# Gate and up products of the second layer's feed-forward stage in two by two blocks with seven half-size products

## Chip, cores, metric

The kernel runs on one core of one Trainium2 chip. The metric is the device time of one execution in microseconds (us). Before the change the median of three runs is 1883.36 us (1878.64 to 1889.82).

## The reference, cut to what matters

A two-layer backbone on 512 latent and 256 context tokens of width 1024. Each layer mixes tokens and then runs a feed-forward stage (FFN) with 2816 hidden columns. The last layer doesn't need its context tokens any more, so its FFN works on the 512 latent tokens alone.

```python
def swiglu(h, w_i, w_o):
    g, u = jnp.split(h @ w_i, 2, axis=-1)
    return (jax.nn.silu(g) * u) @ w_o
...
        xl = xl + ml[2] * rms_norm(yl, g[1])
        xl = xl + ml[5] * rms_norm(swiglu(adaln(xl, g[2], ml[3], ml[4]), w_ffn_in[l], w_ffn_out[l]), g[3])
```

All numbers are float32.

## The kernel before

**Three matmuls for one product.** TensorE runs in the float32r form. Every operand is kept as two parts: `hi`, the value as ScalarE rounds it to float32r, and `lo`, what is left, subtracted by VectorE. A product is hi·hi + hi·lo + lo·hi, so `mm3` issues three matmuls into one PSUM bank. TensorE wants 128 rows (kc runs over eight such blocks of the width 1024).

**Memory.** One SBUF arena is cut into regions, which the profile names reg0, reg1 and so on. In the second layer's FFN reg0 and reg1 hold the normed activations H2 (hi and lo), reg2 the products `silu(g)*u` of the four hidden blocks ("slots") of a group, hi and lo, reg3 scratch, reg4 and reg5 the output rows that are summed up over the groups, reg7 five weight slots (hi and lo, 1024 columns each) and reg8 three raw buffers for weights as they come from HBM, besides small things.

**Weights.** SyncE's queue (SP) fetches all weights through the three raw buffers in one fixed list (`build_seq`), 512 KB each. `pump` turns a raw buffer into a weight slot, in the list's order: ScalarE copies 1024 columns to hi, VectorE subtracts to lo, and the raw buffer goes to the next fetch. A weight slot comes free when its last matmul has been issued (`done`).

**The FFN** (`ffn`). The 22 hidden blocks are taken in groups of 4, 4, 4, 4, 2 and 4. For each block `unit` makes gate and up, each as 8 kc times 3 matmuls of 128x512 (48 for both), then silu on ScalarE, the multiply on VectorE, and the split into hi and lo. After the blocks of a group come its down products: for each of four tiles of 128 tokens and each half of 512 output columns, the group's blocks times three matmuls of 128x512. VectorE adds them to the output rows. The first group begins with two blocks in halves of 256 tokens, since their tiles come out of the stage ahead one by one. In the first layer the same is done for 768 tokens, as 512 and 256.

**The gates.** `gate` spreads the modulation column over rows: four transposes of 128x128 on TensorE into a spare bank, then a copy by ScalarE, for each half of 512. The first layer has four such steps (latent and context), the second two. They are queued at the fourth group.

**Order.** One Python generator emits TensorE's work, and side lanes emit the rest when a clock that the builder keeps says that it is due. What comes out is one fixed order on each engine, and each engine runs its own order strictly.

Of the kernel before, what the change touches and what calls it, by code (L numbers as in the profile page):

```python
# [18 lines left out]
CTX = 256  # L19
# [131 lines left out]
class Builder:  # L151
    def __init__(self, tc, ctx, ins, out):
# [7 lines left out]
        cuts = [A0, A0 + 6144, B0, B0 + 6144, C0, VB, X0, W0, RAW0, self.L.end]  # L160
        self.reg = [[a, b, None, None] for a, b in zip(cuts, cuts[1:])]
        for i, k in enumerate('rrfffffrf'):
            self.mode(i, k)
        self.M = gp.tile([128, 7, 128], U8, name="M")
# [6 lines left out]
        self.narrow = False  # L171
# [20 lines left out]
    def V(self, off, *dims, p0=0, np_=128):  # L192
        a, b, t = self.find(off)
        t0 = t[:, off - a:off - a + 1]
        ps = t0.ap[0][0]
        return bass.AP(t0.tensor, t0.offset + p0 * ps, [[ps, np_]] + [list(d) for d in dims])
# [26 lines left out]
    def mm(self, out, lhsT, rhs, start=True, stop=True):  # L223
        n, m = self.cols(rhs), self.cols(lhsT)
        if rhs.dtype == F32R:
            t = max(0.417 * n, 105)
# [9 lines left out]
        self.nc.tensor.matmul(out, lhsT, rhs, start=start, stop=stop)  # L236

    def mm3(self, out, lh, ll, rh, rl, start, stop):
        r = self.r
        self.mm(out, r(lh), r(rh), start, False)  # L240
        self.mm(out, r(lh), r(rl), False, False)
        self.mm(out, r(ll), r(rh), False, stop)
# [119 lines left out]
    groups = [4, 4, 4, 4, 2, 4]  # L362

    def build_seq(self):
# [15 lines left out]
        for l in range(DEPTH):  # L380
# [23 lines left out]
            for gi, g in enumerate(self.groups):  # L404
                for i in range(2 * f, 2 * (f + g)):
                    w(I['wfi'][l, i])
                    if l == 0 and i > 3 and spread:
                        raw(spread.pop(0), 'g')
                for i in range(f, f + g):
                    w(I['wfo'][l, i])  # L410
                if l == 0:
# [3 lines left out]
        self.seq, ns = [], 0  # L415
        for a, k in seq:
            self.seq.append([a, k, ns, None])
            ns += k == 'w'
# [5 lines left out]

    def pump(self, upto=-1):
        seq, go = self.seq, True
        while go:
            go = False
            if self.n_dma < len(seq) and self.slots:
                it = seq[self.n_dma]  # L430
                it[3] = RAW0 + self.slots.pop(0) * 1024
                self.dma(self.S(it[3], 1024), it[0])
                self.n_dma += 1
                go = True
            while self.n_proc < self.n_dma and seq[self.n_proc][1] != 'w':
                self.n_proc += 1
            if (self.n_proc < self.n_dma and seq[self.n_proc][2] < self.n_freed + NW
                    and (self.n_proc <= upto or self.ck.written(self.S(seq[self.n_proc][3], 1024)) <= self.now + 200)):
                it = seq[self.n_proc]
                w = W0 + (it[2] % NW) * 2048  # L440
# [1256 lines left out]
```

## Time and profile before

| what | value |
| --- | --- |
| median of three runs | 1883.36 us (1878.64 to 1889.82) |
| the profiled execution's own time | 1883.15 us |
| its span | 1881.0 us |
| TensorE (PE) busy | 1812.2 us, 96% |
| VectorE (DVE) busy | 1040.1 us, 55% |
| ScalarE (ACT) busy | 684.0 us, 36% |
| GpSimd (POOL) busy | 208.1 us, 11% |

Busy time of TensorE counts a matmul from its start to its modelled end, so that it says little of how fast matmuls follow each other. For that one counts them between two starts. The second layer's FFN reaches from about 1500 us to the end.

### The profile page before, as it was taken

The numbers are of one execution on the slowest core, as the hardware profiler recorded it, in microseconds if no ns is written. First come the engines' busy times: TensorE is split into PE (matmuls) and PEld (weight loads), VectorE is DVE, ScalarE is ACT, GpSimd is POOL, SyncE is SP. The second block draws the span as 40 slices with busy tenths as digits, with TensorE's granted clock in tenths as the row PEclk, the third lists the DMA queues.
The fourth block names the chain that finished last, engine by engine and source line by source line (L and its number), as shares of the span: only waits on it lengthen the run. The fifth ranks groups of instructions, "written<-read, shape, count | busy, mean of one in ns | idle before, by whom it ended". The sixth has DMA issues, their size and how long they took to land.

```text
span 1881.0 us, 27410 instructions
## 1 busy us (share of the span) xinstructions
PE 1812.2 (96%) x11140; PEld 1507.5 (80%) x11140; DVE 1040.1 (55%) x1781; ACT 684.0 (36%) x1374; POOL 208.1 (11%) x287
## 2 busy tenths in 40 slices
PE   6999999997999999999999999999998989999998
PEld 3888886676789888888888878888776788888886
DVE  3478853566475666555455374887476542433444
ACT  4533431357473221212212264333266543222222
POOL 0000003234220000000000040000434100000002
PEclk9999999998999999999999999999999999999999
DMA  9211118442123433434343212111431223243221
GB/s 343 68 57 35 35 53 202 143 83 62 52 106 99 148 124 112 149 120 144 110 144 107 68 45 72 52 46 57 90 79 33 69 88 101 70 121 101 90 90 56
DMA packets 52782, 179.88 MB, mean 96 GB/s; under 512 B 6960, under 2 KB 7856, under 8 KB 52656
## 3 DMA queue, kind: packets, MB, share of 16 engines
q1 hardware_dynamic: 48816, 169.48, 28.3%
q0 software_dynamic: 3840, 8.65, 3.3%
q8 instruction: 87, 1.43, 0.3%
q14 instruction: 39, 0.32, 0.1%
HBM read 167.36 MB, written 2.10 MB: 90 GB/s over the span
## 4 chain that ended last, share of the span: by engine, by line
PE 85%; DVE 5%; ACT 5%; DMA 2%; issue 1%; POOL 1%; SPq 0%; DVEq 0%; POOLq 0%; ACTq 0%
PE P L236 82%; PE P L246 3%; ACT reg1f L257 1%; ACT reg3f L257 1%; DVE reg8f L959 1%; ACT reg7r L257 1%; DVE reg7r L264 1%; ACT reg8f L257 1%; DMA reg4f<-in_wmod 0%; DMA reg8f<-in_wmod 0%; DMA reg0r<-reg5r 0%; DVE reg4f L264 0%; DMA reg8f<-in_wout 0%; ACT reg0r L257 0%; DVE reg8f L276 0%
## 5 line engine op out<-in xcount | busy, mean ns | idle before, releaser
L236 PE MATMUL P<-reg2r,reg7r 128*128 128x256 f32 (+1 forms) x1920 | 481.0, 338 | 0.2 <-ACT reg8f L257 0.2
L236 PE MATMUL P<-reg0r,reg7r 128*128 128x512 f32 (+1 forms) x1344 | 380.3, 363 | 3.9 <-ACT reg0r L257 3.9
L264 DVE TENSOR_TENSOR reg7r<-reg8f,reg7r 128x1024 fp32r<-128x1024 f32 x200 | 243.1, 1225 | 232.7 <-ACT reg7r L257 231.1
L236 PEld LDWEIGHTS P<-reg2r,reg7r 128*128 128x128 f32 x1920 | 330.2, 190 | 39.1 <-issue 0.7
L257 ACT ACTIVATE reg7r<-reg8f 128x1024 fp32r<-128x1024 f32 x204 | 212.8, 1053 | 369.0 <-issue 150.8
L236 PE MATMUL P<-reg7r,reg0r 128*128 128x512 f32 (+1 forms) x1272 | 328.5, 389 | 8.1 <-ACT reg0r L257 6.1
L236 PE MATMUL P<-reg3r,reg7r 128*128 128x512 f32 (+1 forms) x960 | 321.9, 335 | 0.4 <-DVE reg3r L264 0.4
L236 PEld LDWEIGHTS P<-reg0r,reg7r 128*128 128x128 f32 x1344 | 243.1, 191 | 52.5 <-issue 8.4
L236 PEld LDWEIGHTS P<-reg7r,reg0r 128*128 128x128 f32 x1272 | 233.2, 190 | 58.0 <-ACT reg0r L257 7.1
L236 PE MATMUL P<-reg1r,reg7r 128*128 128x512 f32 (+1 forms) x672 | 241.3, 359 | 0.6 <-DVE reg1r L264 0.6
L236 PE MATMUL P<-reg7r,reg2r 128*128 128x512 f32 (+1 forms) x912 | 231.4, 382 | 5.6 <-DVE reg3r L276 1.9
L236 PEld LDWEIGHTS P<-reg7r,reg2r 128*128 128x128 f32 x912 | 165.7, 188 | 39.4 <-ACT reg2r L257 2.3
L236 PEld LDWEIGHTS P<-reg3r,reg7r 128*128 128x128 f32 x960 | 182.4, 190 | 18.5 <-issue 0.7
L236 PEld LDWEIGHTS P<-reg1r,reg7r 128*128 128x128 f32 x672 | 128.3, 191 | 18.7 <-DVE reg1r L264 1.1
L276 DVE SCALAR_TENSOR_TENSOR reg8f<-reg8f 128x512 f32<-128x512 f32 (+3 forms) x154 | 87.6, 569 | 10.6 <-DMA reg8f<-in_wmod 7.7
L236 PE MATMUL P<-reg7r,reg1r 128*128 128x512 f32 (+1 forms) x240 | 90.6, 378 | 0.1
L959 DVE TENSOR_REDUCE reg8f<-P 128x1 f32<-128x768 f32 (+1 forms) x80 | 67.5, 846 | 30.3 <-PE P L236 30.1
L284 POOL TENSOR_TENSOR reg8f<-reg8f 128x1 f32<-128x1 f32 (+2 forms) x102 | 60.2, 592 | 182.5 <-ACT reg5f L257 98.5
L257 ACT ACTIVATE reg3f<-P,reg8f 128x768 f32<-128x768 f32 (+3 forms) x96 | 52.6, 569 | 59.2 <-DVE reg8f L959 46.8
L257 ACT ACTIVATE reg0r<-reg1f 128x256 fp32r<-128x256 f32 (+1 forms) x46 | 23.5, 511 | 135.4 <-DVE reg1f L264 135.4
L236 PE MATMUL P<-reg7r,reg3r 128*128 128x512 f32 (+1 forms) x192 | 70.0, 364 | 0.0
L257 ACT ACTIVATE reg3f<-P 128x512 f32<-128x512 f32 (+2 forms) x106 | 45.1, 442 | 65.5 <-PE P L246 34.7
(218 smaller groups left out, 2012.0 us busy)
## 6 DMA issues: line engine op xcount, KB each, us to landing
reg8f<-in_wfi SPq DMA_DIRECT2D x88, 512.0 KB, 3.6
reg8f<-in_wmod SPq DMA_DIRECT2D x80, 512.0 KB, 3.7
reg8f<-in_win SPq DMA_DIRECT2D x56, 512.0 KB, 3.6
reg8f<-in_wfo SPq DMA_DIRECT2D x44, 512.0 KB, 3.6
reg8f<-in_wout SPq DMA_DIRECT2D x16, 512.0 KB, 4.2
reg6f<-in_xin SPq DMA_DIRECT2D x12, 512.0 KB, 6.3
reg2r<-reg5r POOLq DMA_DIRECT2D x24, 192.0 KB, 6.0
reg2f<-in_wmod SPq DMA_DIRECT2D x8, 512.0 KB, 6.4
```

The costliest lines, as they stand in the source:

```text
L236: self.nc.tensor.matmul(out, lhsT, rhs, start=start, stop=stop)
L246: self.nc.tensor.transpose(out, in_, self.S(self.L.ident, 128))
L257: self.nc.scalar.activation(out=out, in_=in_, func=func, **kw)
L264: self.nc.vector.tensor_tensor(out=out, in0=a, in1=b, op=op)
L276: self.nc.vector.scalar_tensor_tensor(out=out, in0=a, scalar=s, in1=b, op0=op0, op1=op1)
L284: self.nc.gpsimd.tensor_tensor(out=out, in0=a, in1=b, op=op)
L959: self.nc.vector.tensor_reduce(out=sm(i, 2 + m), in_=x, axis=AX.X, op=ALU.min)
```

## The change

Three things change in the code.

**Blocks.** In the second layer (`fast = (1,)`), from the second group on, `pair` takes gate and up of a hidden block together as one product of a two by two block matrix (gate and up, by the two halves of the 1024 input columns) with another (the two halves of the input columns, by the two halves of 256 tokens). It is made with seven half-size products instead of eight (Winograd's form of Strassen's rule), each of 4 kc and 3 matmuls of 128x256: 84 for both gate and up. In PSUM three of them are added on top of a product that has been read already. Four sums of weight blocks (`sums`, and one in `split_s2`, 512 columns each) are made for every hidden block, and four sums of activation blocks (T1 to T4, `tblocks`) once. `sum2` gives a sum to POOL or to VectorE, as the builder's clock has it. A hidden block now takes four weight slots instead of two: the hi and lo splits are 3584 columns instead of 2048. T4 is written over a block that the first group still reads, so it is made when the second group begins.

**Splits.** For the whole program the lo subtraction is no longer emitted right behind the hi copy, but once the builder's clock has the copy done (`flush`), so VectorE's order changes in many places. Scratch and gate change places in the arena, and the regions are cut finer: reg7 is now reg9, reg8 is reg10, and in the second layer's FFN H2 lies in reg0 to reg2, the hidden blocks in reg3, T2 and the gate in reg4, scratch in reg5, the output rows in reg6 and reg7.

**Down products and gates.** The first tile of a group takes the last hidden block of both halves at its end, the last tile takes both halves side by side. The gates are queued in the last group: in the second layer within the last pair, in the first layer ahead of the last group's down products, where TensorE's own work waits until they are done.

```diff
+    fast = (1,)
...
+                seq.append((I['wfi'][l, i], 'ab'[i % 2] if gi and l in self.fast else 'w'))
...
+            elif k == 'b':
+                ab = [first, i]
+                self.task(0, self.split_a11, ab[:1])
+                self.task(None, self.sums, ab)
+                self.task(None, self.split_s2, ab)
+                self.task(0, self.split, ab[:1])
+                self.task(0, self.split_s4, ab[:1], ab[:1])
+                self.task(0, self.split, ab[1:], ab[1:])
...
+    def sum2(self, out, a, b, op):
+        n = self.cols(out)
+        if max(self.ck.t['po'], self.now) + 2.4 * n < max(self.ck.t['dv'], self.now) + 1.4 * n + 700:
+            self.pool(out, a, b, op, 2.36 * n)
+        else:
+            self.tt(out, a, b, op)
+    def sums(self, w, a, b):
+        a, b, tmp = self.raw(a), self.raw(b), self.S(self.L.u, 512)
+        a11, a21, a22 = self.S(a, 512), self.S(b, 512), self.S(b + 512, 512)
+        yield max(self.ck.written(self.S(k, 1024)) for k in (a, b)) if not self.lows else 1e12
+        self.sum2(a11, a11, a21, ALU.subtract)
+        self.sum2(tmp, a22, a11, ALU.subtract)
+        self.sum2(a21, a21, a22, ALU.add)
+    def split_s2(self, w, a, b):
+        tmp = self.S(self.L.u, 512)
+        yield self.ck.written(tmp)
+        self.halves(w, 512, tmp, 512, lambda: self.sum2(tmp, self.S(self.raw(a) + 512, 512), tmp, ALU.subtract))
...
+            t1 = self.S(TS + 1920, hw)
+            while self.n_t < 3:
+                yield self.now + 500
+            for kc in range(4):
+                diff(at(B21, kc), at(T2, kc))
+                yield self.ck.t['dv']
+                put(T4, kc, t1)
+                yield self.ck.t['dv']
+            self.n_t = 4
...
+            z = self.get()
+            ba, bb = self.bank(), self.bank()
+            yield from prod(z, B11, ba, True)
+            self.act(c1, self.B(ba, hw))
+            yield from prod(z + 512, T2, bb, True)
+            self.done()
+            if last:
+                self.mode(ra + 1, 'f')
+                self.sides[1].append(self.gate(l, 5, G5))
+            yield lambda: not slot or slot - 1 in mul_
+            self.tt(q6, c1, self.B(bb, hw), ALU.add)
+            y, w4, x = self.get(), self.get(), self.get()
+            bc = self.bank()
+            yield from prod(x, T1, bc, True)
+            yield lambda: not slot or put_.get(slot - 1) == 2
+            self.act(p5, self.B(bc, hw))
+            yield from prod(y + 512, B21, ba, False)
+            self.act(s1, self.B(ba, hw), AF.Silu)
+            yield from prod(y, T3, bb, False)
+            self.done()
+            self.tt(u3, c1, self.B(bb, hw), ALU.add)
+            yield from prod(w4, B22, bc, False)
+            self.done()
+            self.tt(q6, q6, self.B(bc, hw), ALU.add)
+            self.sides[2].append(late())
+            yield lambda: self.n_t == 4
+            bd = self.bank()
+            yield from prod(x + 512, T4, bd, True)
+            self.done()
+            self.tt(u3, u3, self.B(bd, hw), ALU.add)
+            self.tt(u3, u3, s1, ALU.mult)
+            self.sides[0].append(put(u3, 0))
...
-            if gi == 3:
-                self.sides[1].append(self.gate(l, 5, G5))
             if last:
-                while self.extra:
+                if not fast:
+                    self.mode(ra + 1, 'f')
+                    self.sides[1].append(self.gate(l, 5, G5))
+                while self.extra and not (fast and (1, 1, 1) in self.have):
                     self.more(force=True)
                 self.nbk = 6 if l else 5
                 yield lambda: not self.sides[1]
...
+                if t == order[0]:
+                    todo = [(nh, i) for nh in range(2) for i in range(g - 1)] + [(nh, g - 1) for nh in range(2)]
+                elif t == order[-1]:
+                    todo = [(nh, i) for i in range(g) for nh in range(2)]
```

`late()` in it adds u3 to p5 (by `sum2`), takes the silu of q6, multiplies, and splits the result into hi and lo; `put` splits.

What this does to the engines' orders is seen at three places. The first is VectorE for one hidden block in the middle of a group of the second layer's FFN. Before, reg3 is scratch, reg2 the hidden block, reg7 the weight slots, reg8 the raw buffers:

```order
L264 TENSOR_TENSOR reg3f<-reg3f,P 128x512
L264 TENSOR_TENSOR reg2r<-reg3f,reg2r 128x512
L264 TENSOR_TENSOR reg7r<-reg8f,reg7r 128x1024 x2
L264 TENSOR_TENSOR reg3f<-reg3f,P 128x512
L264 TENSOR_TENSOR reg2r<-reg3f,reg2r 128x512
```

After, with scratch in reg5, the hidden block in reg3, weight slots in reg9 and raw buffers in reg10:

```order
L267 TENSOR_TENSOR reg10f<-reg10f 128x512
L267 TENSOR_TENSOR reg3r<-reg5f,reg3r 128x256 x2
L267 TENSOR_TENSOR reg5f<-reg5f,P 128x256
L267 TENSOR_TENSOR reg9r<-reg10f,reg9r 128x512
L267 TENSOR_TENSOR reg9r<-reg10f,reg9r 128x1024
L267 TENSOR_TENSOR reg5f<-reg5f,P 128x256 x2
L267 TENSOR_TENSOR reg9r<-reg10f,reg9r 128x512
L267 TENSOR_TENSOR reg9r<-reg10f,reg9r 128x1024
L267 TENSOR_TENSOR reg5f<-reg5f 128x256
L267 TENSOR_TENSOR reg5f<-reg5f,P 128x256
L267 TENSOR_TENSOR reg5f<-reg5f 128x256
L267 TENSOR_TENSOR reg9r<-reg10f,reg9r 128x512
```

In place of four instructions a block VectorE has fourteen: one sum of raw weights, five lo splits of weights, four adds out of PSUM, two multiplies or adds in scratch and two lo splits of the block. The other three sums of 512, and one add of 256, stand on POOL.

The second place is VectorE in the first such block of the second group, which began before with the same rows as above. Now lo splits of T4 (written to reg1) and sums for it (out of reg2) stand among the block's own work:

```order
L267 TENSOR_TENSOR reg5f<-reg5f,P 128x256
L267 TENSOR_TENSOR reg9r<-reg10f,reg9r 128x512
L267 TENSOR_TENSOR reg5f<-reg5f,P 128x256
L267 TENSOR_TENSOR reg1r<-reg5f,reg0r 128x256
L267 TENSOR_TENSOR reg5f<-reg5f,reg2r 128x256
L267 TENSOR_TENSOR reg5f<-reg5f 128x256
L267 TENSOR_TENSOR reg1r<-reg5f,reg0r 128x256
L267 TENSOR_TENSOR reg3r<-reg5f,reg3r 128x256
```

The third row reads the bank of the block's sixth product; the last two of T4's four lo splits stand behind it, and the seventh product reads T4.

The third place is TensorE in the first layer, where the gates stand. Before, they lie among the down products of the fourth group (reg7 are weight slots, reg0 the hidden blocks, the 128x128 rows out of reg8 the transposes of the gate steps and one of the modulation's own):

```order
L246 MATMUL P<-reg8f 128x128 x4
L236 MATMUL P<-reg7r,reg0r 128x512 x6
L246 MATMUL P<-reg8f 128x128 x4
L236 MATMUL P<-reg7r,reg0r 128x512 x12
L246 MATMUL P<-reg8f 128x128 x4
L236 MATMUL P<-reg7r,reg0r 128x512 x108
```

After, they lie between the last group's hidden blocks and its down products (reg3 and reg5 are H2 in this layer, reg9 the weight slots, reg10 where the modulation lies):

```order
L239 MATMUL P<-reg5r,reg9r 128x256
L239 MATMUL P<-reg3r,reg9r 128x256
L249 MATMUL P<-reg10f 128x128 x16
L239 MATMUL P<-reg9r,reg0r 128x512 x72
L249 MATMUL P<-reg10f,reg2f 128x128 x8
```

The sixteen transposes of the four gate steps now stand in one piece, with no other matmul between them, and the down products of the last group wait behind them.

More of the change, by code (lines that the diff above doesn't have):

```diff
@@ L193, in V @@
         a, b, t = self.find(off)
+        assert off + sum((n - 1) * st for st, n in dims) < b
         t0 = t[:, off - a:off - a + 1]
@@ L423, in build_seq, with raw, halves, low @@
         self.n_hi = 0
+    def raw(self, k):
+        return self.seq[k][2]
+    def halves(self, w, o, x, n, then=None):
+        hi, lo = self.S(w + o, n), self.S(w + 1024 + o, n)
+        if self.n_proc >= self.n_hi:
+            self.act(self.r(hi), x)
+        def low():
+            if self.sides[2] and self.nbk == 2 and self.ck.t['po'] + 1200 < self.ck.t['dv']:
+                self.pool(self.r(lo), x, hi, ALU.subtract, 2.36 * n)
+            else:
+                self.tt(self.r(lo), x, hi, ALU.subtract)
+            if then:
+                then()
+        self.lows.append([hi, low, (), self.n_proc + 1])
@@ new lines, in flush, with task @@
+    def flush(self, upto):
+        while self.lows and (self.lows[0][3] <= upto or self.ck.written(self.lows[0][0]) <= self.now + 150):
+            _, low, frees, _ = self.lows.pop(0)
+            low()
+            for k in frees:
+                self.slots.append((self.raw(k) - RAW0) // 1024)
+    def task(self, new, fn, needs, frees=()):
+        if new is not None:
+            self.ends.append(0)
+        self.tasks.append((len(self.ends) - 1, fn, needs, frees))
+        self.ends[-1] = len(self.tasks)
@@ new lines, in ffn, with pair, soon, put @@
+        put_, mul_ = {}, set()
+        def pair(slot, last):
+            c1, q6, u3, p5, s1 = [self.S(TS + k * hw, hw) for k in range(5)]
+            at = A + slot * 1536 + o1
+            def soon(x):
+                return self.ck.written(x) - 250
+            def put(x, o):
+                hi, lo = self.S(at + o, hw), self.S(at + 768 + o, hw)
+                yield soon(x)
+                self.act(self.r(hi), x)
+                yield soon(hi)
+                self.tt(self.r(lo), x, hi, ALU.subtract)
+                put_[slot] = put_.get(slot, 0) + 1
+            def late():
+                self.sum2(p5, p5, u3, ALU.add)
+                yield soon(q6)
+                self.act(q6, q6, AF.Silu)
+                yield soon(q6)
+                self.tt(p5, p5, q6, ALU.mult)
+                mul_.add(slot)
+                yield from put(p5, hw)
+            def prod(w, b, bk, first):
+                yield self.ck.free(bk) if first else max(v for e, v in self.ck.bank.get(bk, {'pe': 0.0}).items())
+                for kc in range(4):
+                    self.mm3(self.B(bk, hw), self.S(w + kc * 128, 128), self.S(w + 1024 + kc * 128, 128),
+                             self.S(b[0] + b[1] * kc, hw), self.S(b[0] + b[1] * kc + b[2], hw), first and kc == 0, kc == 3, not first)
+                    if kc % 2:
+                        yield
+            z = self.get()
[30 more added lines that the diff above has]
+            self.sides[0].append(put(u3, 0))
@@ L1429, in ffn @@
                     self.more()
+        while self.extra:
+            self.more(force=True)
     def ffn_fin(self, t, yo, G5, TS, l, H):
```

257 lines of the change are left out of this document (174 added, 83 removed).

## The prediction

> **What bounds the kernel now.** I read the page first, then the second layer's FFN alone. On the page TensorE (PE) is busy nearly all the time at the full granted clock (PEclk in tenths, 40 slices):
>
> ```profile
> span 1881.0 us, 27410 instructions
> PE 1812.2 (96%) x11140; PEld 1507.5 (80%) x11140; DVE 1040.1 (55%) x1781; ACT 684.0 (36%) x1374; POOL 208.1 (11%) x287
> PEclk9999999998999999999999999999999999999999
> ```
>
> Busy time alone doesn't show that nothing is lost. So I took the FFN's stretch from 1540 to 1870 us in the view by windows, PE's waits in it, and its longest piece in the chain of waits:
>
> ```profile
> 1540.00:1870.00 330.00, 329.17 (x1455) 271.60 (x1454) 127.84 (x143) 90.81 (x120) 8.05 (x11) 1.00 0.30 94
> PE P L236 <- ACT reg2r L257: 0.8, 1, 0.8
> 1539.81 212.51 PE P L236 x937
> ```
>
> The columns of the first row are PE, weight load, DVE, ACT, POOL, clock, DMA. PE waits once, for 0.8 us, and otherwise 937 matmuls of 128x512 follow each other in 212.51 us: 0.2268 us each. DVE works 128 of 330 us, POOL 8. The stage is bound by the number and width of its matmuls, and the other engines have room. What the change saves on PE comes off the time, as long as nobody makes PE wait.
>
> **What the seven products save.** The new matmuls are 128x256. Such matmuls, with the same alternation of hi and lo weights, stand at the start of this stage, in the first halves (timeline of PE):
>
> ```profile
> 1503.23 0.28 PE L236 MATMUL P<-reg1r,reg7r 128*128 128x256 f32 x1
> ...
> 1507.91 0.28 PE L236 MATMUL P<-reg1r,reg7r 128*128 128x256 f32 x1
> ```
>
> Between these two lie 13 threes, 39 matmuls in 4.68 us: 0.120 us each. One hidden block cost 48 x 0.2268 = 10.89 us and will cost 84 x 0.120 = 10.08 us, 0.81 less. 18 of 22 blocks are taken this way: -14.5 us. That is all there is to gain, 0.8% of the time. It would be nothing at 0.1296 us a matmul (10.89 / 84).
>
> The Trainium skill (TensorE: Matmul & The Clock Gate, "Back-to-back issue gap") gives the isolated warm gap as N / 2.4 + 2.5 ns; by that estimate 109.2 and 215.8 ns would save 1.19 us a block and 21.3 us in all. The trace has about 11 ns more on either width, so the sum goes by its rows.
>
> **What DVE and POOL must do beside it.** Durations by form, with the idle time before each group behind the bar: 512 and 1024 columns on DVE and ACT and the fetches from 1540 to 1870 us, 256 columns on DVE from 1500 to 1533, POOL from the whole span:
>
> ```profile
> L264 DVE TENSOR_TENSOR reg7r<-reg8f,reg7r 128x1024 fp32r<-128x1024 f32 x58 | 70.3, 1224 | 80.6 <-ACT reg7r L257 80.6
> L264 DVE TENSOR_TENSOR reg2r<-reg3f,reg2r 128x512 fp32r<-128x512 f32 x20 | 13.9, 693 | 14.0 <-ACT reg2r L257 14.0
> L264 DVE TENSOR_TENSOR reg3f<-reg3f,P 128x512 f32<-128x512 f32 x20 | 13.7, 687 | 62.7 <-PE P L236 62.7
> L264 DVE TENSOR_TENSOR reg2r<-reg3f,reg2r 128x256 fp32r<-128x256 f32 x3 | 1.3, 425 | 1.5 <-ACT reg2r L257 1.5
> L264 DVE TENSOR_TENSOR reg3f<-reg3f,P 128x256 f32<-128x256 f32 x3 | 1.3, 419 | 9.4 <-PE P L236 7.5 <-ACT reg3f L257 2.0
> L257 ACT ACTIVATE reg7r<-reg8f 128x1024 fp32r<-128x1024 f32 x58 | 60.2, 1052 | 121.4 <-issue 85.6 <-PE P L236 18.0 <-DMA reg8f<-in_wfi 10.3
> L257 ACT ACTIVATE reg2r<-reg3f 128x512 fp32r<-128x512 f32 x20 | 12.6, 632 | 92.4 <-DVE reg3f L264 92.4
> L284 POOL TENSOR_TENSOR reg8f<-reg8f,reg6f 128x512 f32<-128x512 f32 x16 | 20.4, 1277 | 41.6 <-PE P L236 40.9
> L284 POOL TENSOR_TENSOR reg3f<-reg3f 128x256 f32<-128x256 f32 x4 | 2.9, 730 | 13.7 <-ACT reg8f L257 7.7 <-DVE reg3f L270 3.6 <-PE P L246 2.4
> reg8f<-in_wfi SPq DMA_DIRECT2D x36, 512.0 KB, 3.6
> ```
>
> By the order of the changed program a block gives DVE four adds out of PSUM (4 x 0.42 = 1.68 us), one sum of 512 (0.69), three lo splits of 512 and two of 1024 (2.08 + 2.45), and four of 256 in scratch and splits (1.70): 8.60 us, of which 6.92 with both inputs in SBUF. POOL gets three sums of 512 and an add of 256: 3 x 1.277 + 0.73 = 4.56 us. PE needs 10.08. Taken alone DVE fits, at 85%. They aren't alone. Three places in the timeline of attention show what happens when the two meet:
>
> ```profile
> 321.11 2.69 POOL L284 TENSOR_TENSOR reg8f<-reg8f,reg6f 128x512 f32<-128x512 f32 x2 [8.12 <-PE P L236]
> ...
> 322.04 0.81 DVE L264 TENSOR_TENSOR reg8f<-reg8f,reg6f 128x512 f32<-128x512 f32 x1
> ...
> 431.70 2.35 POOL L284 TENSOR_TENSOR reg7r<-reg8f,reg7r 128x1024 fp32r<-128x1024 f32 x1 [1.86 <-ACT reg7r L257]
> ...
> 432.73 1.33 DVE L276 SCALAR_TENSOR_TENSOR reg8f<-reg8f 128x1 f32<-128x1 f32 x1
> ...
> 465.01 0.22 DVE L276 SCALAR_TENSOR_TENSOR reg8f<-reg8f 128x1 f32<-128x1 f32 x1
> 465.27 1.02 DVE L276 SCALAR_TENSOR_TENSOR reg3f<-reg3f,reg8f 128x768 f32<-128x768 f32 x1
> 465.67 1.09 POOL L284 TENSOR_TENSOR reg3f<-reg3f,reg8f 128x256 f32<-128x256 f32 x1
> ...
> 469.27 0.62 POOL L284 TENSOR_TENSOR reg3f<-reg3f,reg8f 128x256 f32<-128x256 f32 x1
> ```
>
> The second is the clearest: a DVE instruction with SBUF inputs that takes 0.22 us takes 1.33 when POOL is at work on 1024 columns: it ends at 434.06, so it was held until 433.84, which is 2.14 us after POOL's start (2.09 ns a column). And POOL's 256 columns take 1.09 instead of 0.62 while DVE is at work. One holds the other up. By 2.09 ns, POOL's four instructions keep DVE's two-input work out for 3 x 1.07 + 0.53 = 3.74 us a block, and only the 1.68 us of PSUM adds can run meanwhile. DVE then needs 8.60 + 3.74 - 1.68 = 10.66 us, 0.58 above PE.
>
> The Trainium skill (SBUF — State Buffer, "Who interferes with whom") says the same of a DVE instruction with two SBUF inputs against a GpSimd instruction that reads SBUF: an exclusive lock, the loser blocks for the whole instruction. The rows above agree that it blocks; whether it is for the whole instruction every time decides the second rival.
>
> How much of this reaches PE? A weight slot has some lead. With 1.44 us a product (12 x 0.120), the slot for a block's fourth weight comes free 8.64 us into the block before, its split ends 1.05 + 1.22 later at 10.91, and it is read at 10.08 + 2.88 = 12.96: 2.05 us of lead, at each of the five groups anew, since DVE catches up in the down products (their eight adds and four splits are 4 x 1.22 + 8 x 0.69 = 10.4 of 96 x 0.2268 = 21.8 us). A raw buffer's round is 3.6 (DMA) + 0.69 + 1.28 + 0.63 + 0.69 + 1.28 + 0.63 + 0.69 = 9.5 of 10.08 us: it too has little to give. So 18 x 0.58 = 10.4 us is the upper end of this term in my forecast and 0 the lower, if the lead swallows it. I take 6, nearer the upper end, since both chains lie this close to 10 us and run in a fixed order. ACT stays below both and isn't counted.
>
> **The other parts.** T1 to T3 lie beside the first group, where DVE has room as in the window above: 0. T4 is made while the second group's first block runs. By the order its last lo split follows the add that reads the sixth product: after 8.64 us come an add, a lo split, a sum, a multiply (4 x 0.42), a hi split on ACT beside the multiply, and a lo split of 0.43, so that T4 is whole at about 10.9, where PE would have ended at 10.08. The seventh product can run three quarters of its course before: about 1.3 us late (0 to 3, with POOL in the way).
>
> The first layer's four gate steps use one spare bank, and stand behind each other now: three times PE waits until ACT has emptied the bank. Before, in the second layer (chain, then timeline):
>
> ```profile
> 1752.31 0.44 PE P L246 x4
> ...
> 1752.32 1.04 ACT L257 ACTIVATE reg7r<-reg8f 128x1024 fp32r<-128x1024 f32 x1
> 1753.26 0.58 ACT L257 ACTIVATE reg3f<-P 128x512 f32<-128x512 f32 x1
> ```
>
> PE had done at 1752.75, ACT at 1753.84, 1.09 us later, behind the weight copy. Clear of that copy a round is 0.58 and some 0.3 of handing over. I take 3 x 0.93 = 2.8 us (1.7 to 4.9, for 0.58 and for 0.58 + 1.05 a round). Nothing covers it: only what stands behind waits. The second layer's two gates lie among other matmuls: 0.
>
> The last tile now ends both halves side by side. The last chain began with one add (1873.03, behind the last matmul) and will have two there, the first partly beside PE: +0.3 (0 to 0.7).
>
> ```profile
> 1873.03 0.70 DVE reg4f L264
> ```
>
> The later lo splits in the whole program can free DVE (80.6 us idle before the 1024 splits in this stage alone) or bring a weight late. PE's waits on weight slots are small:
>
> ```profile
> PE P L236 <- DVE reg7r L264: 1.4, 3, 1.0
> PE P L236 <- ACT reg7r L257: 0.7, 1, 0.7
> ```
>
> So at most 2.1 us can go, and about as much can come: 0.
>
> **The sum.** -14.5 + 6.0 + 1.3 + 2.8 + 0.3 = -4.1 us on the profiled execution's 1883.15 us (its span 1881.0 and 2.15 around it; 0.2 below the runs' median): 1879 us. About 0.5%, 9.4 us, is what a measurement of this kernel can tell from no change. The forecast by itself runs from -14.5 + 4.4 = -10.1 (no wait in the blocks) to -14.5 + 10.4 + 3.0 + 4.9 + 0.7 + 2.1 = +6.6, 1873 to 1890.
>
> **Rivals.** First, the lead holds: POOL mostly finds DVE in a PSUM add or waiting, and no block makes PE wait; the later splits bring their 2.1 us. For it speaks that DVE is idle 61% of this stage today. Against it, 10.66 over 10.08. 1883.15 - 14.5 + 4.4 - 2.1 = 1871 us.
>
> Second, and slower: the two engines exclude each other for the whole instruction, in the blocks of the second layer's FFN. Then DVE and POOL need 8.60 + 4.56 = 13.16 us a block; with half of the PSUM adds hidden 12.32, 2.24 above PE, 40.3 us over 18 blocks, less five leads of 2.05: 30 us. 1883.15 - 14.5 + 4.4 + 30 = 1903 us. For it speaks the instruction of 1.33 us, which ended with POOL's; against it, the DVE instruction at 322.04, which lies within POOL's 2.69 us and takes 0.81 instead of 0.69. The change turns into a loss where a block's waiting passes 0.56 us (10.1 / 18), and into one that can be measured at 1.08.
>
> Third, the half-width matmuls don't keep 0.120 us when three banks are added to and the weights change for each product. At 0.135 us a block would be 11.34 us, 18 x 0.45 = 8 above before: 1883.15 + 8 + 4.4 + 6 = 1902. The rows of both layers' 128x256 matmuls speak against it.
>
> **Chances.** Forecast 0.48, first rival 0.27, second 0.22, third 0.03. The forecast's lowest edge is faster by over 0.5%, its rest within. Faster 0.28, same 0.47, slower 0.25. The range leaves out what lies below the first rival's value by more than a microsecond and about half of the slower cases: 1870 to 1901 us.
>
> **What the changed profile would show.** From the second group on, threes of 128x256 at 0.36 us, and 10.08 us from one block's first matmul to the next one's where nothing waits. Each excess there should have DVE or ACT on a weight slot as its releaser, and DVE instructions of more than their 0.69 and 1.22 us next to POOL's. PE waits on reg1 in the second group's first block (T4), and three times about 0.9 us on a copy by ACT between the first layer's last blocks and down products. I am wrong if blocks without a wait take longer than 10.1 us, if DVE's and POOL's instructions keep their lengths when they meet, or if time moves by more than 3 us ahead of the first layer's gates.

## The result, and the profile after

| | median | runs | profiled execution | span |
| --- | --- | --- | --- | --- |
| before | 1884.11 us | 1878.64 to 1889.82 (4) | 1883.15 us | 1881.0 us |
| after | 1908.23 us | 1906.86 to 1908.98 (4) | 1906.86 us | 1905.1 us |

The ratio is 1.0127, with a 95% interval of 1.0096 to 1.0158: slower by 24 us, outside the range. First the page after, then its window of the second layer's FFN and PE's waits in that window:

```profile
PE 1809.0 (95%) x11788; PEld 1533.5 (80%) x11788; DVE 1160.3 (61%) x1987; ACT 740.4 (39%) x1516; POOL 334.1 (18%) x396
```

```profile
1540.00:1870.00 330.00, 304.06 (x2003) 278.43 (x2003) 229.95 (x333) 139.68 (x247) 111.63 (x96) 0.98 0.28 93
```

```profile
PE P L239 <- DVE reg5f L267: 11.0, 8, 1.7
PE P L239 <- DVE reg3r L267: 6.8, 4, 2.3
PE P L239 <- ACT reg3r L260: 3.6, 2, 3.3
PE P L239 <- ACT reg0r L260: 3.6, 2, 2.1
PE P L239 <- DVE reg1r L267: 1.0, 1, 1.0
```

On the page DVE is at 61%, POOL at 18%, and in the stage, too, no engine beside PE is full: DVE works 230 of 330 us, POOL 112. Yet PE now waits 26.0 us by these rows, where it waited 0.8. Not one of them names a weight slot (reg9). PE waits for the adds into scratch (reg5), which read its banks, for the hidden blocks (reg3), and for T4 (reg0 and reg1).

Where the time lies is seen from the first matmul of each group's down products on, in the timeline of PE. From the second group's to the third's it was 65.30 us before (1620.16 to 1685.46). After it is 67.93 (1632.59 to 1700.52), and four blocks at 10.08 would have made it 62.06.

| stretch, by the first down product of each group | before, us | after, us | with 0.81 a block saved |
| --- | --- | --- | --- |
| first to second group (T4) | 65.33 | 73.51 | 62.09 |
| second to third | 65.30 | 67.93 | 62.06 |
| third to fourth | 65.33 | 67.86 | 62.09 |
| fourth to sixth (6 blocks) | 100.25 | 105.71 | 95.39 |

The waits, and what hangs on them, cost 11.4 + 5.9 + 5.8 + 10.3 = 33.4 us, against 14.6 saved. 26.0 us of it are the waits above; part of the rest is PE's clock, which was granted at 0.98 over this window and at 1.00 before.

One block of the third group shows how. This is its timeline; the three rows with reg4r are three blocks' T2 products, so that from one to the next is one block:

```profile
1658.24 1.60 PE L239 MATMUL P<-reg4r,reg9r 128*128 128x256 f32 x12
1668.32 1.60 PE L239 MATMUL P<-reg4r,reg9r 128*128 128x256 f32 x12
1669.06 0.68 DVE L267 TENSOR_TENSOR reg9r<-reg10f,reg9r 128x512 fp32r<-128x512 f32 x1
1669.83 3.16 POOL L287 TENSOR_TENSOR reg10f<-reg10f 128x512 f32<-128x512 f32 x2 [2.89 <-DVE reg9r L267]
1671.15 0.69 DVE L267 TENSOR_TENSOR reg10f<-reg10f 128x512 f32<-128x512 f32 x1 [1.41 <-POOL reg10f L287]
1671.76 1.85 DVE L267 TENSOR_TENSOR reg3r<-reg5f,reg3r 128x256 fp32r<-128x256 f32 x2
1673.53 0.41 DVE L267 TENSOR_TENSOR reg5f<-reg5f,P 128x256 f32<-128x256 f32 x1
1673.99 0.38 PE L239 MATMUL P<-reg0r,reg9r 128*128 128x256 f32 x1 [1.19 <-DVE reg5f L267]
1675.25 1.99 DVE L267 TENSOR_TENSOR reg9r<-reg10f,reg9r 128x1024 fp32r<-128x1024 f32 x1 [0.26 <-ACT reg9r L260]
...
1679.85 1.60 PE L239 MATMUL P<-reg4r,reg9r 128*128 128x256 f32 x12
...
1683.20 0.69 DVE L267 TENSOR_TENSOR reg10f<-reg10f 128x512 f32<-128x512 f32 x1 [1.40 <-POOL reg10f L287]
```

Blocks take 10.08 us where nothing waits (1658.24 to 1668.32), then 11.53. T2's bank is full at 1669.92, and DVE could read it. But next in DVE's order is its sum of raw weights, which needs POOL's first sum. DVE stands still for 1.41 us, sums, and then splits the hidden block: 1.85 us for two instructions of 0.42, while POOL is at its second sum. Only at 1673.53 comes the add that reads the bank, and PE, which wants to add the fifth product onto that bank, goes on at 1673.99. DVE's sum comes again 12.05 us later (1671.15 to 1683.20): that is DVE's round, against PE's 10.08.

The chain of waits leads over a fetch:

```profile
1675.25 2.00 DVE reg9r L267
...
1677.31 3.60 DMA reg10f<-in_wfi
...
1681.12 0.69 DVE reg9r L267
```

A lo split frees the raw buffer, the fetch takes 3.60, then come a lo split, POOL's sum and DVE's. But the fetch isn't what DVE stands still for. It has landed by 1680.91, and DVE works almost without a pause from 1677.16 up to the lo split at 1681.12. In the group's first block no fetch had landed for 20 us before that split, and DVE stands still just as long:

```profile
1659.43 3.17 POOL L287 TENSOR_TENSOR reg10f<-reg10f 128x512 f32<-128x512 f32 x2 [16.30 <-DVE reg9r L267]
1660.76 0.69 DVE L267 TENSOR_TENSOR reg10f<-reg10f 128x512 f32<-128x512 f32 x1 [1.41 <-POOL reg10f L287]
```

POOL's first sum overwrites the columns that this lo split reads, DVE's sum reads what POOL writes, and in DVE's order split and sum mostly stand side by side. So DVE stands still for the whole of POOL's sum, whenever the weights come: 18 times from 1540 to 1870 us, 25.8 us in all. The round closes over DVE's order: behind the sum stand the hidden block's splits, behind these on ACT the copy that waits for them and the next hi copies, and then the lo split at 1687.28, 12.03 us after the first.

### The profile page after: what moved, and what is told of

The parts are those of the page before. It is cut to its first block, busy times and chain, and to the rows that moved or that the text cites. A ratio compares the mean times of both kernels' runs of the same rounds, so it can differ in the third digit from the quotient of the medians.

```text
span 1905.1 us, 29284 instructions
## 1 busy us (share of the span) xinstructions
PE 1809.0 (95%) x11788; PEld 1533.5 (80%) x11788; DVE 1160.3 (61%) x1987; ACT 740.4 (39%) x1516; POOL 334.1 (18%) x396
## 3 DMA queue, kind: packets, MB, share of 16 engines
q8 instruction: 92, 1.51, 0.3%
## 4 chain that ended last, share of the span: by engine, by line
PE 74%; DVE 11%; ACT 6%; DMA 3%; POOL 3%; issue 2%; SPq 0%; DVEq 0%; POOLq 0%; ACTq 0%
PE P L239 72%; PE P L249 3%; DVE reg9r L267 2%; DMA reg10f<-in_wfi 2%; POOL reg10f L287 2%; DVE reg10f L1043 1%; ACT reg9r L260 1%; DVE reg5f L267 1%; POOL reg5f L287 1%; ACT reg4f L260 1%; ACT reg5f L260 1%; DVE reg3r L267 1%; DVE reg8f L279 1%; DVE reg10f L279 1%; ACT reg10f L260 1%
## 5 line engine op out<-in xcount | busy, mean ns | idle before, releaser
L239 PE MATMUL P<-reg3r,reg9r 128*128 128x256 f32 (+1 forms) x1920 | 482.8, 339 | 0.0
L239 PE MATMUL P<-reg0r,reg9r 128*128 128x256 f32 (+1 forms) x1632 | 365.0, 313 | 19.4 <-DVE reg5f L267 11.0
L260 ACT ACTIVATE reg9r<-reg10f 128x1024 fp32r<-128x1024 f32 (+1 forms) x258 | 246.3, 965 | 349.6 <-PE P L239 248.4
L267 DVE TENSOR_TENSOR reg9r<-reg10f,reg9r 128x1024 fp32r<-128x1024 f32 (+1 forms) x251 | 294.8, 1182 | 124.3 <-ACT reg9r L260 122.4
L239 PEld LDWEIGHTS P<-reg3r,reg9r 128*128 128x128 f32 x1920 | 330.9, 190 | 39.3 <-issue 0.7
L239 PE MATMUL P<-reg9r,reg0r 128*128 128x512 f32 (+1 forms) x1272 | 328.6, 390 | 6.2 <-ACT reg0r L260 5.6
L239 PEld LDWEIGHTS P<-reg0r,reg9r 128*128 128x128 f32 x1632 | 272.0, 193 | 45.7 <-DVE reg5f L267 12.6
L239 PEld LDWEIGHTS P<-reg9r,reg0r 128*128 128x128 f32 x1272 | 234.9, 191 | 54.5 <-ACT reg0r L260 6.2
L239 PE MATMUL P<-reg9r,reg3r 128*128 128x512 f32 (+1 forms) x912 | 235.7, 386 | 15.4 <-DVE reg3r L267 6.8
L239 PE MATMUL P<-reg4r,reg9r 128*128 128x256 f32 (+1 forms) x696 | 191.1, 321 | 0.0
```

The lines of the kernel that those rows point to most:

```text
L260: self.nc.scalar.activation(out=out, in_=in_, func=func, **kw)
L267: self.nc.vector.tensor_tensor(out=out, in0=a, in1=b, op=op)
```

## The experiments

Ratios are to the kernel before, measured on the same chip, with 95% intervals. The runs lie on several chips (the kernel before took 1883.14 to 1885.27 us on four of them), so two changed kernels are compared by their ratios where the difference is small.

**The blocks taken out.**

```diff
-    fast = (1,)
+    fast = (9,)
```

> The two by two blocks are taken out of the changed kernel, its other edits stay (later lo splits in the whole program, the gates in the last group of both layers, the new order of down products). My theory: all of the loss behind 1500 us comes from the blocks, and the program-wide edits cost only what the trace shows ahead of there (+1.9 us at 1500) and at the first layer's gates, which is in that sum; the second layer's two gates now stand in one piece too and cost 2 x 0.93. So 1884.1 + 1.9 + 1.9 = 1888 us (1885 to 1891). Rival: the later splits make the weights late in the second layer's FFN too, so that part of the loss stays: 1895 us or more.

Measured: 1888.73 us, 1.0025 (1.0010 to 1.0041), as forecast. From the second layer's FFN on, its profile loses 4.2 us to the kernel before, the change 23.0: most of the loss there, 18.8 us, comes from the blocks.

**No sum on POOL.**

```diff
     def sum2(self, out, a, b, op):
         n = self.cols(out)
-        if max(...) < max(...):
-            self.pool(out, a, b, op, 2.36 * n)
-        else:
-            self.tt(out, a, b, op)
+        self.tt(out, a, b, op)
```

> Every sum of the blocks (weights and activations) goes to DVE, none to POOL; nothing else is edited. My theory (DVE and POOL shut each other out, and DVE waits for a sum of POOL's at the head of its queue, so that DVE's round is 12.05 us a block against 10.08 on PE): DVE has 7.5 us of work back to back a block in the trace and gets 3 x 0.60 + 0.34 more, 9.6 us, and no POOL beside it. The waits in the blocks and at the group ends go nearly all: 1880 to 1889 us. Rival (DVE simply has too much work and POOL relieves it): 2.1 us a block more on a round of 12.05, so 18 x 2.1 = 38 us more at most, 1915 to 1946. Second rival (the fetches and the three raw buffers set the round): 1905 to 1910, unchanged.

Measured: 1886.97 us, 1.0024 (1.0012 to 1.0037), about 20 us faster than the change. DVE in the same block:

```profile
1661.28 2.02 DVE L267 TENSOR_TENSOR reg10f<-reg10f 128x512 f32<-128x512 f32 x3
1663.21 0.75 DVE L267 TENSOR_TENSOR reg3r<-reg5f,reg3r 128x256 fp32r<-128x256 f32 x2
1663.88 0.41 DVE L267 TENSOR_TENSOR reg5f<-reg5f,P 128x256 f32<-128x256 f32 x1
...
1665.54 1.22 DVE L267 TENSOR_TENSOR reg9r<-reg10f,reg9r 128x1024 fp32r<-128x1024 f32 x1
...
1671.49 2.02 DVE L267 TENSOR_TENSOR reg10f<-reg10f 128x512 f32<-128x512 f32 x3
```

The same two splits take 0.75 instead of 1.85, the 1024 columns 1.22 instead of 1.99, and DVE's round is 10.21 (1661.28 to 1671.49). DVE did more work in less time. That fits both POOL's hold on DVE and DVE's standing still for POOL, so the two had to be told apart.

**The engines by themselves.** Short loops with a common start, on buffers of their own (a program of its own, so there is no diff).

> None of the reference is computed: short loops of instructions on buffers of their own, with a common start. DVE 12 adds of 128x512 alone, POOL 8 alone, then 24 on DVE beside 8 on POOL; the same beside DVE adds out of PSUM, beside lo splits of 1024, and beside ACT copies; 256 columns at the end. My theory (a POOL add keeps DVE's work with two SBUF inputs out for its whole length, and the other way round): DVE's 24 adds alone would be 24 x 0.60 = 14.4 us; beside POOL the stretch lasts as long as both together, 14.4 + 8 x 1.1 = about 23 us, and adds out of PSUM keep their 14.4 us. Rival (the engines only share a rate, or meet by chance of the order): the 24 adds take 14.4 to 17 us beside POOL.

The timeline: DVE alone, POOL alone, both, then both with DVE reading PSUM, then ACT alone and beside POOL:

```profile
13.17 8.62 DVE L40 TENSOR_TENSOR dv<-dv 128x512 f32<-128x512 f32 x12
...
22.27 10.64 POOL L44 TENSOR_TENSOR po<-po 128x512 f32<-128x512 f32 x8 [21.82 <-ACT dv L60]
...
33.28 24.94 DVE L40 TENSOR_TENSOR dv<-dv 128x512 f32<-128x512 f32 x24 [11.49 <-ACT dv L60]
33.39 13.38 POOL L44 TENSOR_TENSOR po<-po 128x512 f32<-128x512 f32 x8 [0.48 <-ACT x L61]
...
67.73 17.28 DVE L48 TENSOR_TENSOR dv<-dv,P 128x512 f32<-128x512 f32 x24 [0.43 <-ACT dv L60]
67.84 10.68 POOL L44 TENSOR_TENSOR po<-po 128x512 f32<-128x512 f32 x8 [21.07 <-ACT x L61]
...
118.47 7.88 ACT L56 ACTIVATE ac<-ac 128x512 f32<-128x512 f32 x12
...
126.55 15.82 ACT L56 ACTIVATE ac<-ac 128x512 f32<-128x512 f32 x24
```

24 adds alone are 2 x 8.62 = 17.24 us, beside POOL 24.94: each of POOL's eight adds takes 7.70 / 8 = 0.96 us from DVE and itself goes from 1.33 to 1.67. Adds out of PSUM and ACT's copies keep their time. So the hold is real, but not for the whole of POOL's add (0.96 of its 1.33 us): both alone are 27.88 us, both together 24.94. Lo splits are held, too. The loop that was meant for splits alone ran beside POOL's adds, and its eight splits of 1024 took 16.63 us; the twelve behind it, nearly without POOL, took 15.73.

**POOL kept busy for nobody.** To the kernel without sums on POOL, four adds a block were given whose result isn't read.

```diff
             self.act(c1, self.B(ba, hw))
+            for _ in range(4):
+                self.pool(self.S(TS + 2560, hw), c1, c1, ALU.add, 600)
```

> The kernel with no sum on POOL, and in each block four adds of 128x256 on POOL added, that read the first product's copy and write scratch that nobody reads. Nothing waits for them. My theory (POOL at work shuts DVE out): DVE's round of 10.21 us a block grows by most of 4 x 0.62, less what runs beside DVE's four adds out of PSUM (4 x 0.34): 1.1 to 2.5 us a block, and less the group's lead of 2: 1897 to 1925, around 1908. Rival (only DVE's wait for a sum of POOL's costs time): POOL's adds hold nobody up, 1885 to 1890.

Measured: 1901.80 us, 1.0090 (1.0076 to 1.0104), against 1.0024 without these adds: about 12 us more. DVE, with POOL and PE:

```profile
1666.31 4.09 POOL L287 TENSOR_TENSOR reg5f<-reg5f 128x256 f32<-128x256 f32 x4 [6.51 <-ACT reg5f L260]
...
1666.90 3.03 DVE L267 TENSOR_TENSOR reg10f<-reg10f 128x512 f32<-128x512 f32 x3
1669.85 1.17 DVE L267 TENSOR_TENSOR reg3r<-reg5f,reg3r 128x256 fp32r<-128x256 f32 x2
1670.94 0.41 DVE L267 TENSOR_TENSOR reg5f<-reg5f,P 128x256 f32<-128x256 f32 x1
...
1671.40 0.39 PE L239 MATMUL P<-reg0r,reg9r 128*128 128x256 f32 x1 [1.36 <-DVE reg5f L267]
```

Three sums take 3.03 instead of 2.02 and the two splits 1.17 instead of 0.75. Work on POOL that nobody waits for holds DVE up all the same, and PE then waits for the add behind the sums, though DVE doesn't stand still for POOL here at all.

**DVE's own sum later.** POOL keeps its sums. DVE's sum is a task of its own, emitted when POOL's is done by the builder's clock.

```diff
+                self.task(None, self.sum_tmp, ab)
...
-        self.sum2(a11, a11, a21, ALU.subtract)
-        self.sum2(tmp, a22, a11, ALU.subtract)
-        self.sum2(a21, a21, a22, ALU.add)
+        self.pool(a11, a11, a21, ALU.subtract, 1208)
+        self.pool(a21, a21, a22, ALU.add, 1208)
+    def sum_tmp(self, w, a, b):
...
+        yield self.ck.written(a11) + 300
+        self.tt(tmp, a22, a11, ALU.subtract)
```

> The changed kernel, POOL keeps its three sums of weights a block; only DVE's own sum, which reads POOL's first one, is emitted later, when POOL's sum is done by the builder's clock, so that DVE doesn't stand still for it (1.41 us a block). If standing still at the head of the queue is a cost of its own, DVE's round goes from 12.05 to about 10.7 us and the time to 1890 to 1895. My theory: POOL's first sum then runs beside DVE's work and keeps it out in its turn (0.96 us for 512 columns in the short loops), so that the round only falls to about 11.6 and the time to 1903 (1898 to 1907).

Measured: 1886.14 us, 1.0008 (0.9996 to 1.0020). My theory falls here: 22 us went where I had expected 5, and more than the 1890 to 1895 us that I had put for the standing still alone. The timeline:

```profile
1651.37 1.60 PE L239 MATMUL P<-reg4r,reg9r 128*128 128x256 f32 x12
1661.45 1.60 PE L239 MATMUL P<-reg4r,reg9r 128*128 128x256 f32 x12
1662.80 1.85 DVE L267 TENSOR_TENSOR reg3r<-reg5f,reg3r 128x256 fp32r<-128x256 f32 x2
1664.57 0.41 DVE L267 TENSOR_TENSOR reg5f<-reg5f,P 128x256 f32<-128x256 f32 x1
1664.90 1.45 DVE L267 TENSOR_TENSOR reg10f<-reg10f 128x512 f32<-128x512 f32 x1
...
1671.53 1.60 PE L239 MATMUL P<-reg4r,reg9r 128*128 128x256 f32 x12
1674.26 1.85 DVE L267 TENSOR_TENSOR reg3r<-reg5f,reg3r 128x256 fp32r<-128x256 f32 x2
1676.50 0.39 PE L239 MATMUL P<-reg0r,reg9r 128*128 128x256 f32 x1 [0.49 <-DVE reg5f L267]
```

The hold is as large as before (the splits still take 1.85, the sum 1.45 instead of 0.69), and DVE's round is 11.46 (1662.80 to 1674.26) and then 11.97, near the 11.6 that I had put and not far below the change's 12.05. But the add out of PSUM now stands ahead of the sum, and PE goes two blocks at 10.08 and waits 0.49. A round over PE's own can be paid from the group's lead, four blocks long, and made up in the down products. What PE can't take is that the add and the last block's splits, which it needs soon, come late.

**All four sums on POOL.** The changed kernel's order but for DVE's own sum, which goes to POOL like the other two: DVE can't stand still for it, and POOL works longer.

```diff
-        self.sum2(a11, a11, a21, ALU.subtract)
-        self.sum2(tmp, a22, a11, ALU.subtract)
-        self.sum2(a21, a21, a22, ALU.add)
+        self.pool(a11, a11, a21, ALU.subtract, 1208)
+        self.pool(tmp, a22, a11, ALU.subtract, 1208)
+        self.pool(a21, a21, a22, ALU.add, 1208)
```

> The changed kernel with all four sums of weights on POOL: POOL works longer beside DVE, and DVE never stands still for a sum, so that none stands ahead of its adds out of PSUM. If it is DVE's place in its order that makes PE wait (the adds out of PSUM behind a sum that can't start), the time falls nearly as far as with the later sum, 1886 to 1893. If it is the sum of DVE's round that counts, that stays near 11.46 - 0.60 + 0.96 = 11.8 us and POOL's four sums in a row come late: 1900 to 1910.

Measured: 1888.51 us, 1.0025 (1.0014 to 1.0037), about 20 us faster than the change. Three ways of keeping DVE from standing still ahead of its adds (no POOL, a later sum, the sum on POOL) give 1886 to 1889.

The length of DVE's round doesn't order these times. In the middle of the third group it is 11.51 us here (1660.06 to 1671.57), 11.46 and 11.97 with the later sum, and 11.64 with POOL kept busy (1666.90 to 1678.54), which is some 12 to 15 us slower than these two. What PE's wait follows in the traces is how long after T2's bank is full the add out of it starts:

| kernel | bank full | add starts | later by, us | PE waits, us |
| --- | --- | --- | --- | --- |
| POOL kept busy | 1667.17 | 1670.94 | 3.77 | 1.36 |
| the change | 1669.92 | 1673.53 | 3.61 | 1.19 |
| all four sums on POOL | 1670.49 | 1673.94 | 3.45 | 0.92 |
| DVE's sum later | 1673.13 | 1676.04 | 2.91 | 0.49 |
| no sum on POOL | 1661.54 | 1663.88 | 2.34 | none |

The wait is each time what goes beyond 2.4 to 2.5 us. That much is free, since PE does two other products (2 x 1.44) before it comes back to the bank, and the add itself takes 0.41.

**T4 left out.**

```diff
-        T2, T4 = (TT, hw, 4 * hw), B12
+        T2 = (TT, hw, 4 * hw)
...
+        T4 = T1
...
-            for kc in range(4):
-                diff(at(B21, kc), at(T2, kc))
...
-                put(T4, kc, t1)
```

> T4's four sums and splits are left out (the seventh product reads T1 in its place, so the output isn't the reference's). The second group took 73.5 us, the third 67.9. My theory: the difference is T4, 5.6 us, so 1902.6 (1901 to 1904.5). Rival: T4's work only takes time that DVE's round loses in this group anyway, 1906 to 1909.

Measured: 1900.94 us, 1.0098 (1.0073 to 1.0123): T4 costs 5.5 us by the ratios and 7.3 by the medians, about what I had put (5.6). Its group went from 73.51 to 66.20.

**The first layer's gates in the fourth group.**

```diff
-                if not fast:
-                    self.mode(ra + 1, 'f')
-                    self.sides[1].append(self.gate(l, 5, G5))
...
+            if gi == 3 and not fast:
+                self.mode(ra + 1, 'f')
+                self.sides[1].append(self.gate(l, 5, G5))
```

> The first layer's gates go back to the fourth group, all else stays. The first layer's last group took 89.66 us against 83.47 before. My theory: the four gate steps in one piece are the whole of these 6.2 us, so 1902 us (1901 to 1904). Rival: most of it is the later lo splits and the order of the down products there, and the gates cost 2.8 us as I had put it: 1905.4 (1904.5 to 1907).

Measured: 1903.87 us, 1.0110 (1.0092 to 1.0128), 3.2 us less by the ratios and 4.4 by the medians, at the upper edge of what I had put. The last group's 6.2 us went, and 1.8 came to the fourth group, where the transposes take PE's time. The three waits, in the changed kernel:

```profile
1065.87 0.65 PE L249 MATMUL P<-reg10f 128*128 128x128 f32 x4 [2.02 <-ACT reg1f L260]
1067.21 0.74 PE L249 MATMUL P<-reg10f 128*128 128x128 f32 x4 [0.69 <-ACT reg1f L260]
1068.64 1.11 PE L249 MATMUL P<-reg10f 128*128 128x128 f32 x4 [0.69 <-ACT reg1f L260]
```

Behind them PE's clock fell as well: 0.83 was granted from 1060 to 1080 us (0.57 from 1067 to 1075), and 1.00 from 1060 to 1080 with the gates in the fourth group.

**Combined, and T4 earlier.** No sum on POOL, the gates back, and T4 begun when the first group's blocks have been issued.

```diff
-            while self.n_t < 3:
+            while self.n_t < 2 or not self.t4_ok:
...
-            if gi == 1 and fast:
-                yield lambda: self.n_t == 2
-                self.n_t = 3
...
+            self.t4_ok = True
```

> No sum on POOL, the first layer's gates back in the fourth group, and T4 made as soon as the first group's last hidden block has been issued, beside that group's down products. My theory: 1887.0 of the run without POOL, less 4.4 (the run with the gates in the fourth group, 1903.87 against 1908.23), less the 4.5 us for which PE waits on T4 in the run without POOL (1.36 + 1.87 + 1.24): 1878 us (1875 to 1880), 0.3% below the kernel before. Rival (T4 beside the down products delays their adds out of PSUM, and the waits come back there): 1881 to 1883.

Measured: 1881.74 us, 0.9983 (0.9975 to 0.9992): faster than before, but 4 us over the forecast. T4 still came late, since T1 to T3 weren't done earlier. PE waits three times within 4.5 us:

```profile
1587.98 0.39 PE L239 MATMUL P<-reg0r,reg9r 128*128 128x256 f32 x1 [0.67 <-ACT reg0r L260]
1589.45 0.39 PE L239 MATMUL P<-reg1r,reg9r 128*128 128x256 f32 x1 [1.08 <-DVE reg1r L267]
...
1591.48 0.58 PE L239 MATMUL P<-reg0r,reg9r 128*128 128x256 f32 x1 [1.53 <-ACT reg0r L260]
```

Then it does 27 matmuls of 128x256 in 5.77 us (1591.48 to 1597.25), 0.214 each instead of 0.120. The window's clock (its last column but two) says the same:

```profile
1580.00:1600.00 20.00, 16.13 (x107) 15.15 (x107) 19.09 (x37) 8.85 (x17) 0.00 (x0) 0.83 0.23 77
```

**Early splits ahead of the second layer's FFN.** To the combined kernel:

```diff
                         self.n_proc += 1
+                        if not (self.in_ffn and self.l in self.fast):
+                            self.flush(self.n_proc)
```

> The combined kernel, with the lo splits right behind their hi copies again as in the kernel before, everywhere but in the second layer's FFN. By the profiles the later splits gain 4 to 9 us up to the first layer's FFN and lose 3 to 5 in the second layer's mixer: they cost or bring about the same, so 1878 plus or minus 4 of the combined kernel's time, and the gain and the loss should both be gone from the profile. Rival: the differences ahead of 1500 us are from run to run, and no edit's; then the profile stands as it was with the combined kernel.

Measured: 1883.25 us, 0.9989 (0.9978 to 1.0000), the same time. The loss is gone: from the first layer's last down products to about 1350 us it takes 277.0 us here, 280.1 before, 276.7 and 278.7 in the two kernels below, which have early splits as well, and 282.3 to 285.0 in the nine kernels with later splits (282.3 and 282.9 in the two of them that have the gates in the fourth group, like the four with early splits). The gain is smaller than I had read it: the first layer's first down product stands at 610.8 to 615.9 us in the four kernels with early splits and at 606.9 to 612.1 in the nine with later ones, which overlap. So the later splits gain some 4 us and lose some 5.

**T1 to T3 on POOL again, beside the first group.** To the kernel above:

```diff
-            def diff(p, q):
-                self.sum2(t1, p[0], q[0], ALU.subtract)
+            def diff(p, q, sm=self.sum3):
+                sm(t1, p[0], q[0], ALU.subtract)
...
-                diff(at(B21, kc), at(T2, kc))
+                diff(at(B21, kc), at(T2, kc), self.sum2)
```

Here `sum3` is the old rule, and `sum2` is always DVE.

> The combined kernel with the early splits ahead of the second layer's FFN, and the sums of T1 to T3 may go to POOL again, beside the first group, where DVE has room by the profile; weights and T4 stay on DVE. In the combined kernel T4 began only at 1575 us, at the end of the first group's down products, since T1 to T3 took until then; PE waited 3.9 us in the second group and ran at a granted clock of 0.83 for some 6 us behind it. My theory: T1 to T3 are done some 10 us earlier, T4 lies beside the down products, and these 6 us go: 1877 us (1875 to 1880). Rival: the first group's DVE work is held up by POOL as elsewhere and T4 begins no earlier: 1881 to 1885.

Measured: 1877.85 us, 0.9970 (0.9954 to 0.9986): 7 us faster than before, the best of all. The stretch with T4 went from 68.9 to 64.5 us.

**All together with the later sum.** POOL keeps its sums of weights, DVE's is emitted later, T4 is on DVE, gates and splits as above.

> What helped, together: POOL keeps its sums of weights, DVE's own sum is emitted later (as in the run with that edit alone), the first layer's gates in the fourth group, T4 early and on DVE, T1 to T3 as the changed kernel has them, splits right behind their copies ahead of the second layer's FFN. From the last combined kernel (1877.85): its first four groups took about 64.2 us each from the third on and its last two together 100.4; with the later sum these were 63.6 and 97.3. So 2 x 0.6 + 3.1 less: 1873.5 us (1871 to 1877). Rival (T4 is late again, since DVE has more to wait for around 1580): 1878 to 1882.

Measured: 1879.46 us, 0.9982 (0.9968 to 0.9996), not the 1873.5 that I had put, and not told apart from the one above. The last two groups gained as forecast (97.4 us against 100.4), but the stretch with T4 lost 3 us again (67.5 against 64.5): the rival's place, but not its reason. T4 was whole in time; PE waits 1.58 us for a weight slot and 1.66 for adds out of PSUM.

## Why the prediction was wrong

**What was right.** Matmuls of 128x256 keep 0.120 us, and a block that doesn't wait takes 10.08 (third rival out). No engine beside PE is full. POOL's and DVE's instructions lengthen each other. T1 to T3 cost little (0 was put): the first group takes 3.1 us more, of which 1.8 is a longer wait at 1522 us that the kernel without blocks has too. The gates cost 3.2 to 4.4 net against 2.8 (1.7 to 4.9), though PE's lower clock behind the three waits wasn't in that sum. The tail cost 1.0, more than its 0.3 (0 to 0.7).

**The step that failed** is "So 18 x 0.58 = 10.4 us is the upper end of this term". The waits in the blocks cost 33.4 - 7.3 (T4) = 26 us. I had summed DVE's time as work plus hold, 8.60 + 3.74 - 1.68 = 10.66, and compared that with PE's 10.08, as if it mattered only how much DVE has to do. Work and hold weren't far off: in the round of 12.05 DVE works 10.0 us, of which about 2.3 are hold (1.51 instead of 0.42, 1.99 instead of 1.22, 1.12 instead of 0.68). What wasn't in the sum is that DVE stands still, 1.41 us a block, for POOL's first sum, which can't start before DVE's own lo split just ahead, and that in DVE's fixed order the hidden block's splits and the add out of PSUM stand right behind. PE needs this add within 2.4 us, and it came after 3.6. The rows for it were there: the order after showed `reg10f<-reg10f` first and `reg5f<-reg5f,P` behind it, and my own raw buffer's round had a lo split and POOL's sum in series. I used that round only to ask whether the buffer comes free in time. The releaser that I named was wrong for the same reason: I expected weight slots, and it was reg5 and reg3.

**The rivals.** The first, that no block makes PE wait, is out by the 26.0 us of waits. The second gave 1903 us and the right sign, and its 12.32 us a block is near the 12.05 of the trace. It was still not the cause by itself: with the later sum the splits were held as long and the time was 1886. Nor do the engines exclude each other for the whole instruction, as it had it (24.94 us together in the short loops, 27.88 one after the other). The Trainium skill (SBUF — State Buffer, "Who interferes with whom") has it that a DVE instruction with two SBUF inputs contends with a GpSimd instruction that reads SBUF, and that one with at most one SBUF input, outside the modes that use two ports, doesn't. The short loops agree with both: 0.96 us lost for each of POOL's adds, nothing lost by adds out of PSUM.

**T4** was put at 1.3 us (0 to 3) and cost 5.5 to 7.3 (7.3 in its own stretch). I had the seventh product run three quarters of its course before it waits. It runs half of it, and then waits for the third quarter's hi and lo and for the last one's hi, since each of T4's four rounds is three sums, given to POOL and DVE by turns, the hi copy on ACT and the lo split on DVE, all in series:

```profile
1594.14 0.39 PE L239 MATMUL P<-reg0r,reg9r 128*128 128x256 f32 x1 [1.43 <-ACT reg0r L260]
1595.49 0.39 PE L239 MATMUL P<-reg1r,reg9r 128*128 128x256 f32 x1 [0.96 <-DVE reg1r L267]
1598.12 0.58 PE L239 MATMUL P<-reg0r,reg9r 128*128 128x256 f32 x1 [2.12 <-ACT reg0r L260]
```

The matmuls behind these waits ran at a lower clock as well (0.91 granted from 1600 to 1620 us).

**The later splits** came to about nothing, as forecast, but as a gain of some 4 us and a loss of some 5, where I had put 2.1 as the most of either. The prediction named a shift of over 3 us ahead of the gates as a sign that it was wrong, and so it was, in that term.

**What stays open.** That DVE's late add and splits cost the time in the blocks is shown from both sides: three edits take most of the loss away, and one brings more than half of it back without any sum on POOL. How much of the 20 to 22 us is the standing still and how much the hold isn't shown: of the 3.61 us by which the add comes late, 1.23 are standing still, and the splits take 1.1 more than without POOL (1.77 against 0.67 from the first to the add). By an estimate from these rows either one taken away would leave about the 2.4 us that are free in this block. A fourth raw buffer wasn't tried; by the row at 1660.76 an earlier fetch wouldn't end the standing still. That the two best kernels differ isn't shown.

## What to carry to other kernels

When work is moved to another engine, look at who reads its result and what stands behind that reader in its engine's order: a reader that can't start holds back everything behind it, however idle its engine is on the page. Sum each engine's round with the time that it stands still, and ask separately where the instructions that the bottleneck needs at once stand in it. When two engines hold each other up, as DVE and POOL do here, giving the slower one a part of the faster one's work can cost more than it takes off.

## What the runs showed of the hardware

- A POOL add of 128x512 takes 0.96 us from a DVE that reads two SBUF inputs, and gets longer itself (1.33 to 1.67 us). DVE adds with an input in PSUM and ACT copies lose nothing beside it.
- Several short waits in a row slow PE beyond their length: after 0.67, 1.08 and 1.53 us within 4.5 us (no sum on POOL, T4 earlier), 27 matmuls ran at 0.214 us instead of 0.120, 2.5 us lost, and the granted clock was 0.53 from 1592 to 1597 us. A single wait went either way: behind one of 2.12 us the clock stayed at 1.00 (1636 to 1656 us after the change), and behind one of 2.02 us at the same place it was 0.91 (1626 to 1646 us with the gates in the fourth group).
